# Layer 1's queries, keys and weighed probabilities are turned by VectorE in squares of 32 that change places through memory

## The chip, the cores and the metric

The kernel runs on one core of a Trainium2 chip. The metric is the device time in microseconds (us), as a median over runs: 1236.18 us for the kernel before, over three runs from 1235.33 to 1237.88. Beside it stands one profiled execution, which has a time of its own; all durations below are read from that one.

## The reference, cut to what matters

A two-layer decoder trunk over 512 tokens of 1024 numbers, in float32. Layer 1, where the change is made, has three groups of dilated causal attention with four heads of 128 each, whose outputs are summed per head with weights that come from the softmax denominators:

```python
DIL_PATTERNS = ((128, 1), (512, 4), (2048, 16))
...
    s = jnp.einsum('brhnqd,brhnkd->brhnqk', qc, kb).astype(jnp.float32) * (dh ** -0.5)
...
    s = jnp.where(valid, s, -jnp.inf)
    lse = jax.nn.logsumexp(s, axis=-1)
    p = jnp.exp(s - lse[..., None])
    o = jnp.einsum('brhnqk,brhnkd->brhnqd', p.astype(vb.dtype), vb)
...
    q = rmsnorm(z[:, :, :, 0], q_gain)
    k = rmsnorm(z[:, :, :, 1], k_gain)
    v = z[:, :, :, 2]
...
    wts = jax.nn.softmax(jnp.stack(lses, axis=0), axis=0)
    o = jnp.sum(wts[..., None].astype(v.dtype) * jnp.stack(outs, axis=0), axis=0)
    return o.reshape(B, S, ODD_MIX) @ w_out
```

A gated MLP with a short convolution follows.

## The kernel before, in words

A product on TensorE (PE) takes its contracted index on the partitions. Queries and keys leave their projection with tokens on the partitions and must be turned so that the head's 128 numbers stand there; probabilities leave the softmax with queries on the partitions and must be turned so that keys stand there. The kernel before turns both on PE, 128x128 at a time, against an identity (`cst`), into a PSUM bank, and ScalarE (ACT) copies the bank to SBUF.

All weight products are made of three PE passes (`hi*hi`, `hi*lo`, `lo*hi`). Weights come from memory in slabs: a DMA from SyncE (SP) fills `raw`, ACT makes `hi` (L179), VectorE (DVE) makes `lo` (L182); each has three buffers. A projection of 512 columns is 96 matmuls of 128x512, four slabs of 24; its four tiles of 128 tokens end at six matmuls from each other in the last slab. Layer 1 runs nine such projections one after the other: q and k of group 0, of group 1, of group 2, then the values v0, v1, v2.

The order of PE's instructions is fixed by hand: `at(delay, fn, tag)` puts a piece of work in a heap that comes due after so many us of estimated PE work, and it is placed between the matmuls of the running projection; `drain(tag)` places all that is left. The other engines' instructions are ordered by a scheduler when the program is built; ACT, DVE, GpSimd (POOL) and SP then each go through their own list strictly in order, waits included.

Names and lines that the steps touch:

- `qk_evict` (L383): for each tile, `norm_scale` (square on ACT L367, sum on DVE L369, the root of it by `rsqrt` with two ACT instructions L214 and L215 and small DVE ones), `qn` on DVE (L388), then `tr` 6.5 us and more later: four transposes on PE (L379) and the ACT copy to `q` or `k` (L397, L399). For layer 1 this is 24 tiles.
- `scores` (L876): PE products of `q` and `k`, masks on DVE (L282), exponentials on ACT (L874) into `PR[g]`.
- `residues` and `factors`: small DMAs by POOL (`d`, `s`, `e`, `f`, L913 to L940) and small DVE instructions that give each group's weight per query and head; when they are issued, `weigh` is put into the heap twelve times.
- `weigh` (L943): DVE multiplies each 128x128 block of `PR` in place (L950), then PE transposes it (L957) and ACT copies it back (L959): 60 blocks in 16 banks.
- `values0` (L985): the values of group 0 change their tokens' order through 16 DMAs by POOL (`vt<-vs`).
- `pv` (L962): per head 15 matmuls of the turned blocks with the values (L972), then `split` to `o1hi` and `o1lo` and the output projection (L350).

The profile writes PR, q, k without their group number.

Of the kernel before, what the change touches and what calls it, by code (L numbers as in the profile page):

```python
# [16 lines left out]
F32 = mybir.dt.float32  # L17
F32R = mybir.dt.float32r
I32 = mybir.dt.int32
AF = mybir.ActivationFunctionType  # L20
# [4 lines left out]
P = 128  # L25
# [3 lines left out]
NT = S // P  # L29
# [100 lines left out]
def trunk_kernel(ctx: ExitStack, tc: tile.TileContext, x, weights, params, lqks, w_a2, consts, out):  # L130
    nc = tc.nc
    V, A, G, T = nc.vector, nc.scalar, nc.gpsimd, nc.tensor
# [6 lines left out]
    dr = ctx.enter_context(tc.tile_pool(name="dr", bufs=1, space=bass.MemoryType.DRAM))  # L139
# [3 lines left out]
    def bank():  # L143
        return ps.tile([P, 512], F32, name="bank")
# [7 lines left out]
    ident = cst[:, C_ID:C_ID + P]  # L152
# [122 lines left out]
    g_odd = prm[:, 34:35]  # L275
# [16 lines left out]
    def at(delay, fn, tag):  # L292
        count[0] += 1
        heapq.heappush(events, (now[0] + delay, count[0], tag, fn))

    def fire():
        while events and events[0][0] <= now[0]:
            heapq.heappop(events)[3]()

    def pe(us):  # L300
        now[0] += us

    def run(steps):
        for us in steps:
            pe(us)
            fire()
# [54 lines left out]
    def heads(v, n=4):  # L361
        return v.rearrange("p (h d) -> p h d", h=n)
# [13 lines left out]
    def transposes(src):  # L376
        pt = bank()
        for h in range(4):
            T.transpose(pt[:, h * P:(h + 1) * P], src[:, h * P:(h + 1) * P], ident)  # L379
        pe(0.43)  # L380
        return heads(pt)

    def qk_evict(dst, gain, nh, r, tag, then=None, put=None):  # L383

        def f(t, ps):
            rr = norm_scale(ps, nh, r(t))
            qn = tmp.tile([P, S], F32, name="qn", bufs=3)
            V.tensor_tensor(out=heads(qn, nh), in0=heads(ps, nh),  # L388
                            in1=rr.unsqueeze(2).to_broadcast([P, nh, 512 // nh]), op=ALU.mult)

            def tr():
                pt = transposes(qn)
                to = dst[:, :, t * P:(t + 1) * P]
                if put is not None:
                    to, pt = put(dst, t), pt.rearrange("p h (t l) -> p h t l", t=NT)
                if gain is None:
                    A.activation(to, pt, AF.Copy)  # L397
                else:
                    A.activation(to, pt, AF.Copy, scale=gain)  # L399
                if then is not None:  # L400
                    then(t)
            at(6.5 + t, tr, tag)
        return f

    def scaled(dst, r, c0=0, n=512, then=None):
# [11 lines left out]
    with tc.tile_pool(name="m0", bufs=1) as m0, tc.tile_pool(name="t0", bufs=2) as t0:  # L417
# [145 lines left out]
        def after_k(t):  # L563
            if t == NT - 1:
                at(1.0, lambda: diff_scores(0), "diff")
# [288 lines left out]
    with tc.tile_pool(name="m1", bufs=1) as m1:  # L854
# [8 lines left out]

        PR = [m1.tile([P, 4, 7, P], F32, name="PR0")] + [m1.tile([P, 4, NT, P], F32, name=f"PR{g}") for g in (1, 2)]
        vts = [m1.tile([P, NT, 512], F32, name=f"vt{g}") for g in range(3)]
        fac = []

        def probs(dst, sc, g, t, h):

            nk = sc.shape[1]  # L870
            m = masks[:, 3 - nk // P:3].rearrange("p a b -> p (a b)") if g == 0 else masks[:, 3 * (g - 1)]
            nm = st[g][:, t, 0, h:h + 1]
            masked(dst, sc, m, nm)
            A.activation(dst, dst, AF.Exp, bias=nm, scale=-1.0, accum_out=st[g][:, t, 1, h:h + 1])  # L874

        def scores(g, t, q, k):  # L876
            ts = slice(t * P, (t + 1) * P)
            if g == 0:
                nk = P if t == 0 else 2 * P
                for hp in range(2):  # L880
                    sc = bank()
                    for h in range(2):
                        o = h * 256
                        T.matmul(sc[:, o:o + nk], q[:, 2 * hp + h, ts], k[:, 2 * hp + h, (t + 1) * P - nk:(t + 1) * P],  # L884
                                 start=(h == 0), stop=(h == 1))
                    pe(8 * nk * PASS)
                    for h in range(2):
                        b0 = max(0, 2 * t - 1)
                        dst = PR[0][:, 2 * hp + h, b0:b0 + nk // P].rearrange("p b k -> p (b k)")
                        probs(dst, sc[:, h * 256:h * 256 + nk], 0, t, 2 * hp + h)  # L890
            else:
                sc = bank()
                for h in range(4):
                    hs = slice(h * P, (h + 1) * P)
                    T.matmul(sc[:, hs], q[:, h, ts], k[:, h, ts], start=(h == 0), stop=(h == 3))  # L895
                pe(0.87)
                for h in range(4):
                    probs(PR[g][:, h, t], sc[:, h * P:(h + 1) * P], g, t, h)
            if t < NT - 1:
                at(5.0, lambda: scores(g, t + 1, q, k), "scores")  # L900
            elif g == 0:
                residues()
            elif g == 2:
                factors()
# [13 lines left out]
        def factors():  # L918

            sn = [s0, st[1], st[2]]  # L920
            mx = m1.tile([P, NT, 4], F32, name="mx")
            V.tensor_tensor(out=mx, in0=sn[0][:, :, 0], in1=sn[1][:, :, 0], op=ALU.min)
            V.tensor_tensor(out=mx, in0=mx, in1=sn[2][:, :, 0], op=ALU.min)
            eg = m1.tile([P, 3, NT, 4], F32, name="eg")
            for g in range(3):
                V.tensor_tensor(out=eg[:, g], in0=mx, in1=sn[g][:, :, 0], op=ALU.subtract)
            A.activation(eg.rearrange("p g t h -> p (g t h)"), eg.rearrange("p g t h -> p (g t h)"), AF.Exp)
            den = m1.tile([P, NT, 4], F32, name="den")
            dt = m1.tile([P, NT, 4], F32, name="dt")
            V.tensor_tensor(out=den, in0=eg[:, 0], in1=sn[0][:, :, 1], op=ALU.mult)  # L930
            for g in (1, 2):
                V.tensor_tensor(out=dt, in0=eg[:, g], in1=sn[g][:, :, 1], op=ALU.mult)
                V.tensor_tensor(out=den, in0=den, in1=dt, op=ALU.add)
            V.reciprocal(den, den)
            for g in range(3):
                V.tensor_tensor(out=eg[:, g], in0=eg[:, g], in1=den, op=ALU.mult)

            G.dma_start(e0, eg[:, 0])
            for r in range(4):
                G.dma_start(f0[32 * r:32 * r + 32], e0.rearrange("(t l) r h -> r l t h", t=NT)[r])  # L940
            fac.extend((f0, eg[:, 1], eg[:, 2]))
            for i in range(12):
                at(10.0 + 3.5 * i, lambda i=i: weigh(i // 4, i % 4), "weigh")  # L943

        def weigh(g, h):

            nb = 7 if g == 0 else 4
            for b in range(nb):
                t = (b + 1) // 2 if g == 0 else b
                V.tensor_scalar(PR[g][:, h, b], PR[g][:, h, b], fac[g][:, t, h:h + 1], None, ALU.mult)  # L950

            def tr():
                for b0 in range(0, nb, 4):
                    n = min(4, nb - b0)
                    pt = bank()
                    for b in range(n):
                        T.transpose(pt[:, b * P:(b + 1) * P], PR[g][:, h, b0 + b], ident)  # L957
                    pe(0.107 * n)
                    A.activation(PR[g][:, h, b0:b0 + n].rearrange("p b k -> p (b k)"), pt[:, :n * P], AF.Copy)  # L959
            at(1.5, tr, "weigh")  # L960

        def pv(h):  # L962

            po = bank()
            n0 = po.rearrange("p (t l r) -> p t r l", t=NT, r=4)
            n12 = by_res(po)
            blocks = [(g, b) for g in range(3) for b in range(7 if g == 0 else 4)]
            for i, (g, b) in enumerate(blocks):
                t, kb = ((b + 1) // 2, b // 2) if g == 0 else (b, b)
                to, w = (n0[:, t], PR[g][:, h, b].rearrange("p (r l) -> p r l", r=4)) if g == 0 else \  # L970
                    (n12[:, t], PR[g][:, h, b])
                T.matmul(to, vts[g][:, kb, h * P:(h + 1) * P], w, start=(i == 0), stop=(i == len(blocks) - 1))  # L972
            pe(0.218 * len(blocks))
            return po

# [16 lines left out]
        for g in range(3):  # L992
            q, k = t8("q"), t8("k")
            put = by_tile if g == 0 else None
            run(tok_gemm(512, nat, qk_evict(q, g_odd, 4, rs1, "scores", put=put), make_rs if g == 0 else None))
            run(tok_gemm(512, nat, qk_evict(k, None, 4, rs1, "scores", after_k(g, q, k), put)))
        for g in range(3):
            if g == 2:
                drain("scores")
# [35 lines left out]
```

## Time and profile before

| what | value |
|---|---|
| median of the runs | 1236.18 us (1235.33 to 1237.88) |
| the profiled execution | 1235.43 us |
| its span in the trace | 1233.6 us |
| PE, DVE, ACT, POOL busy | 99%, 62%, 44%, 1% |
| PE's granted clock | full in all 40 slices |

The span runs from the first to the last instruction of the trace; 1.8 us of the execution's time lie around it. In layer 1, the projections of queries and keys begin near 605 us, the last scores end near 788 us, the values of head 0 are gathered from 835 us, and the output projection begins at 848.63 us.

### The profile page before, as it was taken

Reading aid. Unit: us, or ns where it says so; the run is one execution under the profiler, and the core shown is the slowest. Engines: PE = TensorE matmul, PEld = TensorE weight load, DVE = VectorE, ACT = ScalarE, POOL = GpSimd, SP = SyncE. Lnnn points to the kernel's source line nnn. Section 1 sums busy time; section 2 is a strip of 40 time slices with the busy share of each in tenths; the row PEclk is TensorE's granted clock in tenths of the full one; section 3 lists DMA queues with packets and bytes.
Section 4 is the critical chain, followed back from the end, with each engine's and each line's share of the span. In section 5 each row is a group of like instructions: output and inputs, shape, how many; then the busy total and the mean of one; then the engine's idle time right before and its main releaser. Section 6 shows DMA issues by size and latency. Waiting matters only on the chain.

```text
span 1233.6 us, 15017 instructions
## 1 busy us (share of the span) xinstructions
PE 1225.8 (99%) x5783; PEld 1014.4 (82%) x5783; DVE 767.2 (62%) x1450; ACT 546.4 (44%) x896; POOL 16.4 (1%) x35
## 2 busy tenths in 40 slices
PE   9999999999999999999999999999999999999998
PEld 7888688788888888888888888889888888888887
DVE  6557868787744775377645654534777537763673
ACT  6446655454422443245545554444544314432441
POOL 0000000000000000000000000300000000000000
PEclk9999999999999999999999999999999999999999
DMA  7222111233333322332422222421232332332322
GB/s 255 87 87 69 52 53 45 92 94 95 103 94 94 103 97 91 103 94 69 138 86 86 73 83 86 121 85 37 101 102 87 102 103 87 101 103 87 102 77 94
DMA packets 34630, 114.54 MB, mean 93 GB/s; under 512 B 4439, under 2 KB 5368, under 8 KB 34560
## 3 DMA queue, kind: packets, MB, share of 16 engines
q1 hardware_dynamic: 32400, 110.38, 28.4%
q10 hardware_dynamic: 1296, 2.10, 0.5%
q0 software_dynamic: 864, 1.12, 0.4%
q8 instruction: 45, 0.74, 0.2%
q14 instruction: 25, 0.20, 0.1%
HBM read 110.41 MB, written 2.12 MB: 91 GB/s over the span
## 4 chain that ended last, share of the span: by engine, by line
PE 97%; DMA 1%; ACT 1%; DVE 1%; SPq 0%; issue 0%; POOL 0%; DVEq 0%; POOLq 0%; ACTq 0%
PE bank L749 39%; PE bank L333 24%; PE bank L791 19%; PE bank L350 7%; PE bank L379 1%; PE bank L972 1%; PE bank L519 1%; PE bank L553 1%; PE bank L957 1%; PE bank L895 1%; PE bank L884 0%; PE bank L541 0%; PE bank L647 0%; PE bank L681 0%; DMA xT<-in_xT_dram 0%; PE bank L612 0%
## 5 line engine op out<-in xcount | busy, mean ns | idle before, releaser
L179 ACT ACTIVATE hi<-raw 128x1024 fp32r<-128x1024 f32 (+2 forms) x209 | 217.1, 1040 | 310.4 <-PE bank L791 143.2
L182 DVE TENSOR_TENSOR lo<-raw,hi 128x1024 fp32r<-128x1024 f32 (+2 forms) x209 | 250.5, 1199 | 141.0 <-ACT hi L179 134.0
L749 PE MATMUL bank<-hhi,hi 128*128 128x512 f32 x704 | 273.9, 389 | 0.0
L749 PE MATMUL bank<-hhi,lo 128*128 128x512 f32 x704 | 273.9, 389 | 0.0
L749 PE MATMUL bank<-hlo,hi 128*128 128x512 f32 x704 | 273.9, 389 | 0.0
L333 PE MATMUL bank<-hi,hhi 128*128 128x512 f32 (+2 forms) x480 | 186.8, 389 | 0.0
L333 PE MATMUL bank<-lo,hhi 128*128 128x512 f32 (+2 forms) x480 | 181.2, 378 | 0.8 <-DVE lo L182 0.8
L333 PE MATMUL bank<-hi,hlo 128*128 128x512 f32 (+2 forms) x480 | 180.5, 376 | 0.0
L749 PEld LDWEIGHTS bank<-hhi,lo 128*128 128x128 f32 x704 | 132.2, 188 | 27.5
L749 PEld LDWEIGHTS bank<-hlo,hi 128*128 128x128 f32 x704 | 132.2, 188 | 27.4
L749 PEld LDWEIGHTS bank<-hhi,hi 128*128 128x128 f32 x704 | 132.2, 188 | 27.4
L791 PE MATMUL bank<-ghi,lo 128*128 128x512 f32 (+1 forms) x358 | 138.0, 385 | 0.0
L791 PE MATMUL bank<-glo,hi 128*128 128x512 f32 (+1 forms) x358 | 138.0, 385 | 0.0
L791 PE MATMUL bank<-ghi,hi 128*128 128x512 f32 (+1 forms) x358 | 138.0, 385 | 0.0
L333 PEld LDWEIGHTS bank<-lo,hhi 128*128 128x128 f32 x480 | 90.2, 188 | 18.4 <-DVE lo L182 1.5
L333 PEld LDWEIGHTS bank<-hi,hhi 128*128 128x128 f32 x480 | 90.5, 188 | 15.9 <-ACT hi L179 0.6
L333 PEld LDWEIGHTS bank<-hi,hlo 128*128 128x128 f32 x480 | 90.5, 189 | 14.9 <-DVE hlo L207 0.3
L796 DVE TENSOR_TENSOR xT<-xT,bank 128x512 f32<-128x512 f32 (+1 forms) x49 | 33.1, 675 | 106.4 <-PE bank L791 106.2
L791 PEld LDWEIGHTS bank<-ghi,lo 128*128 128x128 f32 x358 | 67.3, 188 | 13.6
L791 PEld LDWEIGHTS bank<-ghi,hi 128*128 128x128 f32 x358 | 67.3, 188 | 13.5
L791 PEld LDWEIGHTS bank<-glo,hi 128*128 128x128 f32 x358 | 67.3, 188 | 13.4
L203 ACT ACTIVATE ghi<-cv 128x512 fp32r<-128x512 f32 x44 | 27.7, 631 | 109.4 <-DVE cv L774 109.4
(201 smaller groups left out, 1340.3 us busy)
## 6 DMA issues: line engine op xcount, KB each, us to landing
raw<-in_weights_dram SPq DMA_DIRECT2D x189, 512.0 KB, 3.5
raw<-in_weights_dram SPq DMA_DIRECT2D x16, 384.0 KB, 3.0
xT<-in_xT_dram SPq DMA_DIRECT2D x7, 256.0 KB, 5.9
out_dram<-xT ACTq DMA_DIRECT2D x7, 256.0 KB, 2.0
raw<-in_weights_dram SPq DMA_DIRECT2D x2, 544.0 KB, 3.5
vt<-vs POOLq DMA_DIRECT2D x16, 64.0 KB, 3.9
raw<-in_weights_dram SPq DMA_DIRECT2D x2, 256.0 KB, 3.1
xT<-in_xT_dram SPq DMA_DIRECT2D x2, 128.0 KB, 3.0
```

What stands on the lines that cost most here:

```text
L179: r = A.activation(hi[:, c0:c1], raw[:, c0:c1], AF.Copy)
L182: V.tensor_tensor(out=lo[:, c0:c1], in0=raw[:, c0:c1], in1=hi.bitcast(F32)[:, c0:c1], op=ALU.subtract)
L203: A.activation(hi, src, AF.Copy)
L333: T.matmul(ps[t][:, :n], lhs(a[:, kc], t), b[:, k, :n], start=(kc == 0 and j == 0), stop=(kc == DC - 1 and j == 2))
L350: T.matmul(ps, w[:, k, d * P:(d + 1) * P], r(k), start=(k == 0 and j == 0), stop=(k == nk - 1 and j == 2))
L379: T.transpose(pt[:, h * P:(h + 1) * P], src[:, h * P:(h + 1) * P], ident)
L519: T.matmul(sc[:, :nk], qT[rs, h, n * P:(n + 1) * P], kT[rs, h, :nk], start=True, stop=True)
L553: T.matmul(po[n][:, h * P:(h + 1) * P], wT[:, j * P:(j + 1) * P], bv[:, j, h * P:(h + 1) * P], start=(h == 0 and j == 0), stop=(h == 3 and ...
L749: T.matmul(ps, w[:, kc], r[:, kc], start=(kc == 0 and m == 0), stop=(kc == DC - 1 and m == 2))
L791: T.matmul(ps[:, ts], a[:, k], b[f0 + k][:, ts], start=(k == 0 and m == 0), stop=(k == n - 1 and m == 2))
L796: V.tensor_tensor(out=xT[:, c, ts], in0=xT[:, c, ts], in1=ps[:, ts], op=ALU.add)
L895: T.matmul(sc[:, hs], q[:, h, ts], k[:, h, ts], start=(h == 0), stop=(h == 3))
```

## The change

Queries, keys and weighed probabilities of layer 1 are no longer turned on PE. `turn` has DVE transpose a tile of 128x512 (or 128x384) inside each square of 32x32, and ACT issues one DMA that writes the result to a buffer in memory. `settle` has POOL issue four DMAs, of 32 partitions each, that read the squares back to the places they have in the turned tile: 128 pieces of 512 (or 384) bytes each. Turned queries and keys arrive in a buffer `z` (three of them), from which ACT copies to `q` and `k` as before; turned probabilities arrive in `PR` itself. The buffer that DVE writes (`turn`) exists twice. What comes due changes with it: the copy to `q` and `k` 11.5 us after the tile and not 6.5, the later scores of group 2 after 4.0 us and not 5.0, and `weigh` in steps of 2.6 us from 6.0 on, head by head (group 1, 2, 0 of head 0, then of head 1, and so on), where it went group by group in steps of 3.5 us from 10.0 on.

```diff
+    def turn(pool, src, n):
+        sq = pool.tile([P, 4, 4, 32], F32, name="turn", bufs=2)[:, :, :n]
+        V.transpose(sq.rearrange("p j b r -> p b j r"), src.rearrange("p (b j c) -> p b j c", b=n, j=4))
+        d = dr.tile([P, 4, n * 32], F32, name=f"turned{n}", bufs=3)
+        A.dma_start(d, sq.rearrange("p j b r -> p j (b r)"))
+        return d.rearrange("(i c) j x -> j c i x", i=4)
+
+    def settle(to, d):
+        for j in range(4):
+            G.dma_start(to[32 * j:32 * j + 32].rearrange("c i b r -> c i (b r)"), d[j])
...
+            if turned is not None:
+                z = turned.tile([P, 4, 4, 32], F32, name="z", bufs=3)
+                settle(z, turn(turned, qn, 4))
+
             def tr():
-                pt = transposes(qn)
...
+                pt = z.rearrange("p i h l -> p h i l") if turned is not None else \
+                    transposes(qn).rearrange("p h (i l) -> p h i l", i=4)
...
-            at(6.5 + t, tr, tag)
+            at((11.5 if turned is not None else 6.5) + t, tr, tag)
...
-                at(5.0, lambda: scores(g, t + 1, q, k), "scores")
+                at(5.0 if g < 2 else 4.0, lambda: scores(g, t + 1, q, k), "scores")
...
             for i in range(12):
-                at(10.0 + 3.5 * i, lambda i=i: weigh(i // 4, i % 4), "weigh")
+                at(6.0 + 2.6 * i, lambda i=i: weigh((1, 2, 0)[i % 3], i // 3), "weigh")
...
-            def tr():
-                for b0 in range(0, nb, 4):
-                    n = min(4, nb - b0)
-                    pt = bank()
-                    for b in range(n):
-                        T.transpose(pt[:, b * P:(b + 1) * P], PR[g][:, h, b0 + b], ident)
-                    pe(0.107 * n)
-                    A.activation(PR[g][:, h, b0:b0 + n].rearrange("p b k -> p (b k)"), pt[:, :n * P], AF.Copy)
-            at(1.5, tr, "weigh")
+            for b0 in range(0, nb, 4):
+                w = PR[g][:, h, b0:min(nb, b0 + 4)].rearrange("p b k -> p (b k)")
+                n = w.shape[1] // P
+                to = w.rearrange("p (i b l) -> p i b l", i=4, b=n)
+                settle(to, turn(m1, w, n))
+                for b in range(n):
+                    turned[g, h, b0 + b] = to[:, :, b]
...
-                T.matmul(to, vts[g][:, kb, h * P:(h + 1) * P], w, start=(i == 0), stop=(i == len(blocks) - 1))
+                T.matmul(to, vts[g][:, kb, h * P:(h + 1) * P], turned[g, h, b], start=(i == 0),
+                         stop=(i == len(blocks) - 1))
...
-            run(tok_gemm(512, nat, qk_evict(q, g_odd, 4, rs1, "scores", put=put), make_rs if g == 0 else None))
-            run(tok_gemm(512, nat, qk_evict(k, None, 4, rs1, "scores", after_k(g, q, k), put)))
+            run(tok_gemm(512, nat, qk_evict(q, g_odd, 4, rs1, "scores", put=put, turned=m1), make_rs if g == 0 else None))
+            run(tok_gemm(512, nat, qk_evict(k, None, 4, rs1, "scores", after_k(g, q, k), put, m1)))
```

Place A: ACT's list where the keys of group 0 are copied, just ahead of the exponentials of the first scores. Before, the four copies come from banks and stand one behind the other:

```order
422 L397 ACTIVATE k<-bank 128x16x32
423 L214 ACTIVATE rs_y_5497<-rs_a_5496 128x4
424 L215 ACTIVATE rs_y_5497<-rs_y_5497 128x4
425 L397 ACTIVATE k<-bank 128x16x32
426 L179 ACTIVATE hi<-raw 128x1024
427 L397 ACTIVATE k<-bank 128x16x32 x2
428 L179 ACTIVATE hi<-raw 128x1024
```

Now, where `z` is the buffer that POOL's DMAs fill:

```order
437 L414 ACTIVATE k<-z 128x16x32
438 L179 ACTIVATE hi<-raw 128x1024
439 L414 ACTIVATE k<-z 128x16x32
440 L367 ACTIVATE sq<-bank,rstd_5160 128x512
441 L214 ACTIVATE rs_y_5678<-rs_a_5677 128x4
442 L215 ACTIVATE rs_y_5678<-rs_y_5678 128x4
443 L414 ACTIVATE k<-z 128x16x32
444 L389 DMA turned_5692<-turn 128x512
```

The last copy of a key tile now stands behind the square `sq` and the root of the first tile of the next queries. On PE the same place reads, now:

```order
2835 L333 MATMUL bank<-hi,hhi 128x512
2836 L333 MATMUL bank<-hi,hlo 128x512
2837 L333 MATMUL bank<-lo,hhi 128x512
2838 L901 MATMUL bank<-k,q 128x128 x4
2839 L333 MATMUL bank<-hi,hhi 128x512
```

The three matmuls ahead of the scores (L901) end the first tile whose `sq` stands ahead of the key copy on ACT; the first scores read all four key tiles, since those of group 0 are stored by residue.

Place D: the end of the values' projection on PE, before (L957 are transposes of weighed probabilities, L972 the gathering of values):

```order
3470 L957 MATMUL bank<-cst,PR_5075 128x128 x4
3471 L333 MATMUL bank<-hi,hhi 128x512
3472 L333 MATMUL bank<-hi,hlo 128x512
3473 L333 MATMUL bank<-lo,hhi 128x512
3474 L333 MATMUL bank<-hi,hhi 128x512
3475 L333 MATMUL bank<-hi,hlo 128x512
3476 L333 MATMUL bank<-lo,hhi 128x512
3477 L957 MATMUL bank<-cst,PR_5075 128x128 x12
3478 L972 MATMUL bank<-PR_5073,vt_5076 128x4x32 x7
```

Now no transpose stands there, and the four heads follow the projection's last matmul:

```order
3443 L333 MATMUL bank<-lo,hhi 128x512
3444 L986 MATMUL bank<-PR_5073,vt_5076 128x4x32 x7
3445 L986 MATMUL bank<-PR_5074,vt_5077 128x128 x4
3446 L986 MATMUL bank<-PR_5075,vt_5078 128x128 x4
3447 L986 MATMUL bank<-PR_5073,vt_5076 128x4x32 x7
3448 L986 MATMUL bank<-PR_5074,vt_5077 128x128 x4
```

POOL's list from the values on, now (`PR_5073` is group 0, `PR_5074` group 1, `PR_5075` group 2; each row is one `settle`, and before the list ended with `f`):

```order
34 L1005 DMA vt_5076<-vs 32x512 x16
35 L955 DMA e_5082<-eg 128x16
36 L957 DMA f_5080<-e_5082 32x4x4 x4
37 L394 DMA PR_5074<-turned_6946 32x4x128 x4
38 L394 DMA PR_5075<-turned_6972 32x4x128 x4
39 L394 DMA PR_5073<-turned_7010 32x4x128 x4
40 L394 DMA PR_5073<-turned_7018 32x4x96 x4
41 L394 DMA PR_5074<-turned_7042 32x4x128 x4
42 L394 DMA PR_5075<-turned_7072 32x4x128 x4
43 L394 DMA PR_5073<-turned_7099 32x4x128 x4
44 L394 DMA PR_5073<-turned_7107 32x4x96 x4
```

The pattern of four rows per head goes on to head 3, and the second half of group 0 is the last of each head, though `pv` reads it among its first rows.

## Rows read from the trace of the kernel before

**Rows 1.** The page: busy us by engine, clock by slice, chain by engine.

```profile
PE 1225.8 (99%) x5783; PEld 1014.4 (82%) x5783; DVE 767.2 (62%) x1450; ACT 546.4 (44%) x896; POOL 16.4 (1%) x35
...
PEclk9999999999999999999999999999999999999999
...
PE 97%; DMA 1%; ACT 1%; DVE 1%; SPq 0%; issue 0%; POOL 0%; DVEq 0%; POOLq 0%; ACTq 0%
```

**Rows 2.** PE's waits: waiter, what it waited for, us in total, times, longest.

```profile
PE bank L224 <- DVE hhi L221: 1.5, 1, 1.5
```

**Rows 3.** Chain of waits, 640 to 700 us: start, us, what.

```profile
639.91 14.75 PE bank L333 x65
654.66 0.44 PE bank L379 x4
...
664.69 0.89 PE bank L884 x8
```

**Rows 4.** Chain of waits, 786 to 872 us, its first row by line.

```profile
by line: PE bank L333 31.8%; PE bank L350 25.3%; PE bank L972 15.6%; PE bank L957 8.5%; DMA f<-e 3.8%; DMA e<-eg 3.5%; POOL f L940 1.9%; PE bank L749 1.8%; ACT PR L874 1.7%; issue 1.6%; DVE lo L182 1.4%; PE bank L895 1.1%; DVE den L933 0.4%
...
786.96 0.90 PE bank L895 x8
...
792.94 3.04 DMA e<-eg
...
796.26 1.65 POOL f L940 x3
797.91 3.25 DMA f<-e
...
801.70 1.50 PE bank L957 x7
...
835.23 13.40 PE bank L972 x120
848.63 21.79 PE bank L350 x96
```

**Rows 5.** Timeline of ACT: start, us, what, idle before.

```profile
625.58 0.69 ACT L367 ACTIVATE sq<-bank,rstd 128x512 f32<-128x512 f32 x1 [0.67 <-PE bank L333]
...
627.75 0.21 ACT L215 ACTIVATE rs_y<-rs_y 128x4 f32<-128x4 f32 x1
```

**Rows 6.** ACT by form, 600 to 850 us: busy us and mean ns of one, idle before.

```profile
L397 ACT ACTIVATE k<-bank 128x512 f32<-128x512 f32 x12 | 7.1, 594 | 13.4 <-PE bank L379 13.4
```

**Rows 7.** DVE by form, 600 to 850 us.

```profile
L182 DVE TENSOR_TENSOR lo<-raw,hi 128x1024 fp32r<-128x1024 f32 x38 | 46.5, 1223 | 76.2 <-ACT hi L179 71.0 <-PE bank L957 5.2
L388 DVE TENSOR_TENSOR qn<-bank,rr 128x512 f32<-128x512 f32 x24 | 16.4, 688 | 0.8
```

**Rows 8.** Timeline of DVE, 792 to 802 us.

```profile
792.51 3.42 DVE L950 TENSOR_SCALAR PR<-PR,eg 128x128 f32<-128x128 f32 x17
```

**Rows 9.** Timeline of POOL, 680 to 830 us.

```profile
778.99 3.96 POOL L990 DMA_DIRECT2D vt<-vs  x8 [85.13 <-ACT vs L988]
```

**Rows 10.** Windows: stretch, its us, PE, PEld, DVE, ACT, POOL busy, clock, DMA, GB/s.

```profile
222.00:224.00 2.00, 1.08 (x4) 0.60 (x5) 1.59 (x2) 0.24 (x1) 0.00 (x0) 1.00 0.04 12
...
224.00:228.00 4.00, 4.00 (x19) 3.28 (x18) 0.93 (x2) 1.00 (x2) 0.00 (x0) 1.00 0.39 125
```

**Rows 11.** Windows while POOL issues four DMAs (`s`, then `f`).

```profile
691.67:693.86 2.19, 2.19 (x12) 1.80 (x11) 0.20 (x1) 0.00 (x0) 2.19 (x4) 1.00 0.37 71
796.26:798.46 2.20, 2.20 (x11) 1.81 (x11) 2.20 (x9) 0.00 (x0) 2.20 (x4) 1.00 0.19 17
```

**Rows 12.** DMA issues: queue, times, KB each, median us to landing.

```profile
xT<-in_xT_dram SPq DMA_DIRECT2D x7, 256.0 KB, 5.9
out_dram<-xT ACTq DMA_DIRECT2D x7, 256.0 KB, 2.0
vt<-vs POOLq DMA_DIRECT2D x16, 64.0 KB, 3.9
...
s<-d POOLq DMA_DIRECT2D x4, 4.0 KB, 5.1
```

More of the change, by code (lines that the diff above doesn't have):

```diff
@@ L381, in transposes, with qk_evict @@
         return heads(pt)
-    def qk_evict(dst, gain, nh, r, tag, then=None, put=None):
+    def turn(pool, src, n):
[7 more added lines that the diff above has]
+            G.dma_start(to[32 * j:32 * j + 32].rearrange("c i b r -> c i (b r)"), d[j])
+    def qk_evict(dst, gain, nh, r, tag, then=None, put=None, turned=None):
         def f(t, ps):
@@ L389, in f @@
                             in1=rr.unsqueeze(2).to_broadcast([P, nh, 512 // nh]), op=ALU.mult)
+            if turned is not None:
+                z = turned.tile([P, 4, 4, 32], F32, name="z", bufs=3)
+                settle(z, turn(turned, qn, 4))
             def tr():
-                pt = transposes(qn)
-                to = dst[:, :, t * P:(t + 1) * P]
-                if put is not None:
-                    to, pt = put(dst, t), pt.rearrange("p h (t l) -> p h t l", t=NT)
+                pt = z.rearrange("p i h l -> p h i l") if turned is not None else \
+                    transposes(qn).rearrange("p h (i l) -> p h i l", i=4)
+                to = put(dst, t) if put is not None else \
+                    dst[:, :, t * P:(t + 1) * P].rearrange("p h (i l) -> p h i l", i=4)
                 if gain is None:
@@ L865, in trunk_kernel @@
         vts = [m1.tile([P, NT, 512], F32, name=f"vt{g}") for g in range(3)]
-        fac = []
+        fac, turned = [], {}
         def probs(dst, sc, g, t, h):
@@ L969, in pv @@
                 t, kb = ((b + 1) // 2, b // 2) if g == 0 else (b, b)
-                to, w = (n0[:, t], PR[g][:, h, b].rearrange("p (r l) -> p r l", r=4)) if g == 0 else \
-                    (n12[:, t], PR[g][:, h, b])
-                T.matmul(to, vts[g][:, kb, h * P:(h + 1) * P], w, start=(i == 0), stop=(i == len(blocks) - 1))
+                to = n0[:, t] if g == 0 else n12[:, t].rearrange("p (i l) -> p i l", i=4)
+                T.matmul(to, vts[g][:, kb, h * P:(h + 1) * P], turned[g, h, b], start=(i == 0),
+                         stop=(i == len(blocks) - 1))
             pe(0.218 * len(blocks))
```

## The prediction

> **What bounds the kernel now.** I read the page first. PE is busy 1225.8 of 1233.6 us and makes 97% of the chain of waits, at the full granted clock (2.4 GHz) in every slice [rows 1]. Its longest wait for anything is 1.5 us, at the start of the first output projection of layer 0 [rows 2]. So the time is the sum of PE's instructions, and what leaves PE leaves the time, unless PE then waits for what came instead. Second, the chain in the projections of layer 1: transposes of a query or key tile stand in it as 0.44 us per four [rows 3]. Third, the chain at the end of the attention: PE again, broken only by the two small DMAs `e` and `f`, during which PE worked on at the values; the weighed probabilities' transposes hold 8.5% of 86.0 us [rows 4]. POOL is nearly idle, 16.4 us in all [rows 1]; the change gives it most of its work, so fourth I read POOL's issues and their landings [rows 9, 11, 12].
>
> **What is removed.** 24 tiles of queries and keys at 0.44 [rows 3]: 10.56 us. The 60 transposes of probabilities: 8.5% of 86.0, 7.3 us [rows 4] (60 at 0.11 would be 6.6; the first group waited for DVE, 1.50 for seven). PE saves 17.9 us, all on the path. ACT loses 16 copies from banks, off the path. The profiled execution took 1235.43, 0.75 below the median of the runs: with nothing late it would become 1217.6, a median of 1218.3.
>
> **What is added, off the path.** DVE gets 40 transposes. The trace has none; an instruction of 128x512 takes 0.69, and four of 128x128 at 0.20 each take 0.8 [rows 7, 8]. I take 0.69, the nearest in shape (bounds 0.2, as one small instruction, and 1.2, as `lo`): 28 us, in an engine idle for 466 [rows 1]. ACT gets 40 DMA issues, each landing perhaps 2.0 after, the time of 256 KB written to memory from ACT's queue [rows 12]. POOL gets four issues per tile: 8 of `vt` took 3.96, 0.495 each, four of `s` 2.19 and of `f` 2.20, 0.55 each [rows 9, 11]. I take 0.55, whose pattern in the buffer has several pieces per partition like the new ones: 2.2 us a tile, 53 for queries and keys and 35 for probabilities. For queries and keys that is 8.8 per projection of 96 matmuls at 0.227 (21.8 us [rows 3]), and the copies come due 5 us later. Cover enough, but for one place.
>
> **Place A, the first scores of group 0.** They read all four key tiles. The last copy stands on ACT behind `sq` and the two root instructions of a tile that PE ends with the very matmul ahead of the scores. From the start of such a `sq` to the end of its second root instruction the trace shows 625.58 to 627.96, 2.4 us [rows 5]; the copy adds 0.6 [rows 6]. PE waits 3.0 (bounds 2.4, if the hand-offs shrink, and 4.2, with one `lo` of 1.2 between on DVE [rows 7]). In groups 1 and 2 the first scores need key tile 0 alone: I find no wait.
>
> **Place D, weighing and gathering.** Let s be the end of the last scores on PE (787.86 before [rows 4]). From there PE has 144 matmuls of the values, 32.7 us, then four heads of 3.35 (13.40 for all [rows 4]), 15 matmuls each. It wants the second half of group 0 after 4 of a head's 15: at s+33.6, 37.0, 40.3 and 43.65.
> - `e` is issued at s+5.1, `f` from s+8.4 and landed at s+13.3 [rows 4]. Group 0 of head 0 can only then be weighed: DVE does five blocks (1.0), a `lo` (1.2), two blocks and the transpose (0.4 and 0.7) [rows 7, 8], then ACT issues and the write lands after 2.0. With hand-offs I put that at s+19.2.
> - POOL has settled groups 1 and 2 of head 0 by then and stood idle some 4 us, because its list has group 0 next. From s+19.2 it has 14 settles of 2.2: head 0 is issued by 23.6, head 1 by 32.4, head 2 by 41.2, head 3 by 50.0. The buffers `turn` don't bind: a transpose, an issue and a landing for two of them are below 2 us a tile.
> - A read of 64 KB lands 3.9 after its issue (`vt`, the same size [rows 12]), so 3.35 after the issue's end: the four heads are complete at 27.0, 35.8, 44.6 and 53.4. Heads 0 and 1 are in time. Head 2 makes PE wait 4.3; head 3, then wanted at 47.95, 5.45 more. Sum 9.75.
>
> ACT also holds the last values' copy behind one DMA issue: 0.3 (0 to 1). After the last head nothing new waits: the output projection begins with heads 0 to 2.
>
> **The sum.** -10.56 - 7.3 + 3.0 + 9.75 + 0.3 = -4.8: 1230.6 beside the profiled 1235.43, a median of 1231.4. For an issue interval i and a landing L the wait at D is 19.2 + 55 i + L - 43.65. Between i 0.495 with L 2.0 and i 0.57 with L 4.5 it is 4.8 to 11.4: 1226 to 1233.
>
> While POOL issued `s`, DVE was busy 0.20 of 2.19 us; while it issued `f`, 2.20 of 2.20, with the weighing itself: four issues took 2.19 and 2.20 [rows 11]. The Trainium skill (SBUF — State Buffer, "SBUF: two separate sides") says that a DMA issued by POOL is starved of descriptors while DVE runs certain SBUF-to-SBUF instructions, and gives 620 ns alone against 3100 beside one. By it, 56 issues would need up to 174 us (an estimate from that page) and the change would be a large loss; this pair of rows shows none of it.
>
> **Rivals.**
> 1. *The queue of eight.* POOL's list lets eight DMAs be under way: each waits for the landing of the one eight before. If L grows, i can't be below L/8. For: a settle moves 128 pieces and `s`, with many small pieces, landed after 5.1; `xT` shows 5.9 when the queues are full [rows 12]. Against: `vt` is as large and took 3.9. At 5.1, i is 0.64, the wait at D 15.7 and the median 1237.3; at 5.9, 0.74, 22.0 and 1243.6. It decides from L = 5.3 on: above, the change is slower by over 0.2%. The Trainium skill (VectorE: DVE Perf Modes, "The three transpose paths") warns of plain DMA copies that transpose by access pattern, 19 times slower than the hardware's own; by it L would be far above 5.9. No run here shows such a copy.
> 2. *The clock falls at place D.* PE idles 2 to 5 us at a time there. For: the trace has no idle so long at full clock. Against: 0.92 us of 2 idle, and the clock stayed at 1.00 there and behind [rows 10]. At the lower level (1.2 GHz) the last 11 gathering matmuls take 2.5 more; a slab of 24 behind them would take 5.5 more. 1233.9 to 1239.4.
> 3. *The settles are hidden*, and only place A waits: i of 0.37 or less, or a walk that starts 10 us earlier. For: nothing in the rows. 1219 to 1225.
> 4. *ACT's list jams.* Its DMA issues wait for DVE and for landings, and `hi` stands behind them. For: 40 new waits in a list kept in order. Against: three buffers of `hi` give PE 8 us and more of slack. Each slab that is late by 2 us costs 2; several, some 6 to 10: 1237 to 1242.
> 5. *POOL starved by DVE* (the same rows speak against it): at most DVE's work in that stretch, some 24 us (14 transposes at 0.69, six `lo`, 35 blocks at 0.20): up to 1255.
>
> **How the numbers follow.** My forecast 0.47 (faster 0.44, within 0.2% 0.03); rival 1 0.23 (within 0.09, slower 0.14); rival 2 0.12 (0.09, 0.03); rival 3 0.10, faster; rival 4 0.05 and rival 5 0.03, slower. Faster 0.54, the same 0.21, slower 0.25; 0.2%, 2.5 us, is about what a measurement of this kernel tells from no change. The range reaches from the middle of rival 3 to the upper end of rival 1: 1222 to 1244.
>
> **What would show it.** PE's waits: the scores of group 0 for ACT's `k`, 3 us; the gathering for POOL's DMAs into PR, near 10 us in heads 2 and 3. POOL's timeline: four issues in 2.2 us, without a pause from the first group 0 on. No rows of L379 in layer 1. The granted clock behind the gathering. I am wrong if POOL's issues there stand apart by more than 0.6 us, if PE doesn't wait at the gathering, or if `lo` or `hi` appear among PE's waits with over 1 us.

## The result, and the profile after

The changed kernel takes 1243.65 us (median of 4 runs, 1241.0 to 1246.0) against 1236.01 for the kernel before, now over four runs: a ratio of 1.0058, 95% interval 1.0046 to 1.0071. It is slower, where 1231.4 and faster was forecast; the time lies inside the stated range. The profiled span grew from 1233.6 to 1241.3 us, by 7.7.

The page after, in the columns of [rows 1]:

```profile
PE 1216.0 (98%) x5627; PEld 1005.4 (81%) x5627; DVE 789.0 (64%) x1490; ACT 538.7 (43%) x880; POOL 103.3 (8%) x195
...
PEclk9999999999999999999998999999999999999999
```

PE lost 156 instructions. Its busy time fell by 9.8 us only, because some of what is left ran at the lower clock; in e10 below, at full clock, it fell by 18.4. PE's waits, where [rows 2] had nothing over 1.5:

```profile
PE bank L901 <- ACT k L414: 6.9, 1, 6.9
PE bank L986 <- DMA PR<-turned: 5.9, 4, 3.1
PE bank L986 <- ACT vt L424: 4.9, 2, 4.0
```

**Place A.** The chain of waits at the first scores of group 0 (start, us, what), against [rows 3]:

```profile
656.86 4.08 DMA turned<-turn
...
663.13 5.70 DMA z<-turned
...
670.07 1.62 POOL z L394 x3
671.69 4.17 DMA z<-turned
675.86 0.02 issue
675.88 0.64 ACT k L414
676.52 0.04 issue
676.56 2.08 PE bank L901 x8
678.64 6.95 PE bank L333 x24
...
694.50 5.45 PE bank L333 x24
```

The last key tile lands at 675.86 and ACT's copy starts at once. On the way POOL's list stood still twice, 1.5 us together, with the next read waiting for the landing of the DMA that had been issued eight before:

```profile
667.76 0.55 POOL L394 DMA_DIRECT2D z<-turned  x1 [0.73 <-DMA z<-turned]
669.11 0.55 POOL L394 DMA_DIRECT2D z<-turned  x1 [0.80 <-DMA z<-turned]
```

Behind the wait the scores take 2.08, where they took 0.89 [rows 3], and the slab behind them 6.95, where later ones take 5.45. The windows there say why (columns as in [rows 10]; the clock is the number after POOL's):

```profile
672.00:676.00 4.00, 0.00 (x0) 0.00 (x0) 3.31 (x8) 1.59 (x5) 0.24 (x1) 0.86 0.75 219
676.00:680.00 4.00, 3.44 (x12) 3.15 (x13) 1.82 (x10) 2.25 (x9) 0.22 (x1) 0.50 0.38 150
680.00:684.00 4.00, 4.00 (x15) 3.21 (x15) 1.05 (x2) 1.38 (x2) 1.95 (x4) 0.78 0.29 70
684.00:688.00 4.00, 4.00 (x20) 3.39 (x19) 3.39 (x17) 2.58 (x9) 0.00 (x0) 1.00 0.11 41
```

While PE idled its clock fell to the lower level (0.50, 1.2 GHz), and from 684 on it read full again. Place A costs 6.9 + 1.2 + 1.5 = 9.6 us; 3.0 was forecast.

**Place D.** PE's timeline, the last scores of group 2 and the gathering (L986):

```profile
793.56 1.05 PE L912 MATMUL bank<-k,q 128*128 128x128 f32 x8
...
827.10 2.62 PE L986 MATMUL bank<-PR,vt 128*128 128x128 f32 x22
833.67 0.80 PE L986 MATMUL bank<-PR,vt 128*128 128x128 f32 x2 [3.95 <-ACT vt L424]
835.46 6.00 PE L986 MATMUL bank<-PR,vt 128*128 128x128 f32 x36 [1.00 <-ACT vt L424]
841.89 1.13 PE L986 MATMUL bank<-PR,vt 128*128 128x128 f32 x8 [0.44 <-DMA PR<-turned]
846.11 4.06 PE L986 MATMUL bank<-PR,vt 128*128 128x128 f32 x22 [3.09 <-DMA PR<-turned]
851.49 1.13 PE L986 MATMUL bank<-PR,vt 128*128 128x128 f32 x8 [1.31 <-DMA PR<-turned]
853.64 2.69 PE L986 MATMUL bank<-PR,vt 128*128 128x128 f32 x22 [1.03 <-DMA PR<-turned]
```

With s at 794.6 the values end at s+32.5 (32.7 worked out). The gathering then takes from 827.1 to 856.3, 29.2 us where 13.40 is its work [rows 4]: 15.8 more, against 10.05 forecast. The clock read 0.66 from 830 to 840, where the 16 DMA engines were busy 0.94 of the time (0.36 in the same stretch before):

```profile
830.00:840.00 10.00, 5.33 (x27) 4.88 (x28) 3.73 (x5) 2.78 (x5) 7.79 (x16) 0.66 0.94 288
```

Between 845 and 850 it read 0.66 again. But the last head's second half starts when its read has landed and runs at full clock, so as this trace reads the falls moved the end little. POOL's timeline, against [rows 9]:

```profile
804.01 1.09 POOL L394 DMA_DIRECT2D PR<-turned  x2
807.48 3.39 POOL L394 DMA_DIRECT2D PR<-turned  x6 [2.38 <-issue]
815.79 4.89 POOL L394 DMA_DIRECT2D PR<-turned  x9 [4.92 <-DMA turned<-turn]
822.09 1.09 POOL L394 DMA_DIRECT2D PR<-turned  x2 [1.42 <-DMA PR<-turned]
...
848.20 3.79 POOL L394 DMA_DIRECT2D PR<-turned  x7 [0.51 <-DMA PR<-turned]
```

It stands idle until group 0 of head 0 has been written (815.79), and then needs 36.2 us for 56 issues, 0.65 each. An issue itself is 0.548, as forecast; nearly all the rest is eight waits for an earlier read's landing, 5.1 us together, and each of them ended within 0.6 us of the landing of the DMA issued eight before. The landings (columns of [rows 12]):

```profile
turned<-turn ACTq DMA_DIRECT2D x36, 256.0 KB, 2.9
z<-turned POOLq DMA_DIRECT2D x96, 64.0 KB, 3.9
PR<-turned POOLq DMA_DIRECT2D x48, 64.0 KB, 4.1
```

The sum by the trace: -17.9 + 9.6 + 15.8 = +7.5 beside the measured 7.7. That the two agree to 0.2 is partly luck: with the 19.1 that e10 shows for the first term the sum would be +6.3.

### The profile page after: what moved, and what is told of

It is laid out like the page before. It is cut to its first block, busy times and chain, and to the rows that moved or that the text cites. A ratio compares the mean times of both kernels' runs of the same rounds, so it can differ in the third digit from the quotient of the medians.

```text
span 1241.3 us, 15085 instructions
## 1 busy us (share of the span) xinstructions
PE 1216.0 (98%) x5627; PEld 1005.4 (81%) x5627; DVE 789.0 (64%) x1490; ACT 538.7 (43%) x880; POOL 103.3 (8%) x195
## 4 chain that ended last, share of the span: by engine, by line
PE 90%; DMA 5%; DVE 2%; POOL 1%; issue 1%; ACT 1%; SPq 0%; DVEq 0%; POOLq 0%; ACTq 0%
PE bank L766 39%; PE bank L808 19%; PE bank L333 18%; PE bank L350 7%; DMA turned<-turn 1%; DMA PR<-turned 1%; DMA z<-turned 1%; PE bank L536 1%; PE bank L570 1%; POOL PR L394 1%; DVE lo L182 1%; PE bank L901 1%; POOL z L394 1%; PE bank L379 1%; PE bank L912 1%
## 5 line engine op out<-in xcount | busy, mean ns | idle before, releaser
L333 PEld LDWEIGHTS bank<-lo,hhi 128*128 128x128 f32 x480 | 90.6, 189 | 17.9 <-DVE lo L182 1.4
L394 POOL DMA_DIRECT2D z<-turned x96 | 52.0, 549 | 516.7 <-DVE rs_a L213 437.5
```

Source lines behind the costliest of these rows:

```text
L333: T.matmul(ps[t][:, :n], lhs(a[:, kc], t), b[:, k, :n], start=(kc == 0 and j == 0), stop=(kc == DC - 1 and j == 2))
L394: G.dma_start(to[32 * j:32 * j + 32].rearrange("c i b r -> c i (b r)"), d[j])
```

## The experiments

Ratios go by the kernel before on the same chip, with the 95% interval in brackets. That kernel took 1236.0 to 1237.4 us in the median on the chips used, so a difference in us between two experiments is good to some 1.5 us. Waits are those of one profiled execution each.

**The parts alone.** e1 takes `weigh` and `pv` from the kernel before, e2 passes no `turned` to `qk_evict`.

```diff
-            run(tok_gemm(512, nat, qk_evict(q, g_odd, 4, rs1, "scores", put=put, turned=m1), ...))   # e2
+            run(tok_gemm(512, nat, qk_evict(q, g_odd, 4, rs1, "scores", put=put), ...))
```

> Only queries and keys go through DVE and memory; the probabilities are weighed and turned as before. Theory (the two places add up: -10.6 of transposes against 9.6 at the first scores, a wait of 6.9 and 2.7 at the lower clock): about -1, 1235, with the same wait of 7 at the first scores of group 0. Rival (the loss at the end of the attention is partly made by the queries' and keys' traffic, or the first scores' wait hides something): under 1232 or over 1239.

> Only the weighed probabilities go through DVE and memory. Theory: -7.3 of transposes against 16 at the gathering: +9, about 1245, with POOL's 56 issues behind the first of group 0 spread over some 36 us. Rival (the first scores' delay is what makes the end late): near 1236.

e1: 1231.16, ratio 0.9957 (0.9943 to 0.9972), with a wait of 6.0 at the first scores. e2: 1239.25, 1.0026 (1.0016 to 1.0036). Queries and keys alone gain 4.9, the probabilities alone lose 3.2, together they lose 7.6: the parts don't add up, and 9 us come from their meeting. The trace of e2 shows the larger part of it. There the last scores end where they did before (787.7), 39.3 us of the values follow them, and the gathering ends at 850.7, 23.8 us after its start:

```profile
786.61 1.05 PE L912 MATMUL bank<-k,q 128*128 128x128 f32 x8
826.95 2.62 PE L986 MATMUL bank<-PR,vt 128*128 128x128 f32 x22
...
837.94 12.78 PE L986 MATMUL bank<-PR,vt 128*128 128x128 f32 x92 [0.73 <-DMA PR<-turned]
```

In the whole change the keys' copies are due 5 us later, 30 matmuls of the values come ahead of the last scores, and the cover for POOL's list (the work on PE between the last scores and the gathering) is 32.5, 6.8 less; the gathering takes 29.2, 5.5 more than in e2. No run changes that cover alone. The expectations for e1 and e2 had taken the places one by one.

**The first scores later.**

```diff
-                    at(2.5 if g == 0 else 1.0, lambda: scores(g, 0, q, k), "scores")
+                    at(8.5 if g == 0 else 1.0, lambda: scores(g, 0, q, k), "scores")
```

> Changed kernel, the first scores of group 0 due 6 us later (one slab of 24 matmuls, 5.46 us, goes ahead of them). Theory T (the last key tile lands late, whatever stands ahead of it): the wait falls from 6.9 to about 1.4, the clock stays at its upper level, 8 us gained: 1235 to 1236. Theory O of the prediction (the copy waits for the square of the tile that PE has just ended): the order moves with it and the wait at the scores stays near 3 or more, or vanishes if ACT's list moves the copy ahead.

> Only queries and keys go through DVE and memory (1231.2 as measured), with the first scores of group 0 due 6 us later. If the 6.0 us wait and the low clock behind it (2 us) are all that place costs, and 1.4 of a new wait comes as in the changed kernel with later scores: 1224 to 1225. If the wait only moves: 1229 or more.

e3: 1236.95, ratio 1.0008 (0.9998 to 1.0018), 6.7 below the changed kernel. The wait for `k` is gone and the clock stays at 1.00; a new one stands among PE's waits:

```profile
PE bank L333 <- DVE qn L401: 1.4, 1, 1.4
```

The clock in the 4 us that hold it:

```profile
676.00:680.00 4.00, 2.56 (x16) 1.97 (x15) 4.00 (x15) 1.79 (x6) 0.53 (x1) 1.00 0.38 98
```

Theory T holds: ACT's copy still starts with the read's landing, 1.3 us after ACT had come free, so the square ahead of it never bound. e8, the same in e1: 1227.36, 0.9923 (0.9908 to 0.9938). That is 9.9 below the kernel before on its chip, where e1 was 4.9 below: 5 more, and not the 6 to 7 expected. The profiled execution (1225.60, a span of 1223.8) comes near the forecast, the median of the runs doesn't, and no trace shows why.

**Whole rows.**

```diff
-        return d.rearrange("(i c) j x -> j c i x", i=4)
+        return d.rearrange("(j c) i x -> j c i x", j=4)
```

> Changed kernel, POOL's reads take whole rows of the buffer in memory, 2 KB a partition in one piece, with the same bytes and the same waits; the squares do not change places, so the output is another. Theory P (the pieces of 512 bytes make the landings long and fill the DMA engines): reads land in 2 to 3 us and not 4, POOL's waits for landings (5.1 us at the end) vanish, the first scores wait 3 to 4 less: 1236 or below. Rival B (bytes and the writes' landings make it): within 2 us of 1243.6.

1242.9, 1.0052 (1.0037 to 1.0067): no change. The reads landed in 3.6 (`z`) and 4.4 (`PR`), against 3.9 and 4.1; POOL still waited 4.0 for landings at the end, in seven waits, and the first scores waited 4.8. Theory P falls: the 512-byte pieces don't make the landings long. The Trainium skill (VectorE: DVE Perf Modes, "The three transpose paths") calls a plain DMA copy that transposes by access pattern 19 times slower than the DMA's own transpose when the innermost stride at its destination is large. Here the innermost run is 512 bytes in one piece, so the warning doesn't reach these reads; the prediction had left out that condition, and no run here shows such a copy.

**Four buffers z.**

```diff
-                z = turned.tile([P, 4, 4, 32], F32, name="z", bufs=3)
+                z = turned.tile([P, 4, 4, 32], F32, name="z", tag="z", bufs=4)
```

> Changed kernel with four buffers z and not three (shared with vs). In the changed kernel POOL's reads of the fourth key tile began 0.5 us after ACT's copy of the first key tile had ended. Theory Z (they wait for that copy, since z has three buffers): they begin when the fourth write has landed, about 1.7 us earlier, the wait at the first scores falls from 6.9 to 5, and the time by 2 to 1241.5. Rival (the landings alone set it): no change.

1243.1, 1.0049 (1.0034 to 1.0064): no change in time. The wait fell to 5.7, but e1 and e6 show 6.0 and 5.9 with three buffers. POOL's last reads of keys now wait for the fourth write:

```profile
668.23 2.17 POOL L394 DMA_DIRECT2D z<-turned  x4 [0.72 <-DMA turned<-turn]
```

Theory Z falls: buffer and write came free within a moment of each other.

**Group 0 last.**

```diff
-                at(6.0 + 2.6 * i, lambda i=i: weigh((1, 2, 0)[i % 3], i // 3), "weigh")
+                at(6.0 + 2.6 * i, lambda i=i: weigh(*((1 + i % 2, i // 2) if i < 8 else (0, i - 8))), "weigh")
```

> Changed kernel, groups 1 and 2 of all heads are weighed before group 0 of any, so that POOL need not wait for the first block of group 0 with nothing to issue. Theory P (POOL's list of 64 issues at about 0.65 us sets the end of the gathering): the last read is issued some 6 us earlier, 1237 to 1238. Rival W (the writes and the two buffers of turn set it, or the waits for the values' copies on ACT): under 2 us gained, or slower.

> The whole change with the first scores of group 0 due 6 us later and group 0 weighed last: the gains of the two alone were 6.7 and 3.8 us. If they add up: 1233. If the earlier last scores only lengthen the wait at the gathering: 1237 or more.

e6: 1239.87, 1.0019 (1.0010 to 1.0029), 3.8 gained, between the two expectations. The waits for `vt` vanish, POOL's last issue is at 846.44 and not 851.4 (1.5 of this because the last scores ended earlier in this execution), and PE waits 9.9 for the reads. e12, with the later first scores as well: 1234.53, 0.9977 (0.9968 to 0.9986): 9.1 of the 10.5 that the two gained alone. The whole change is then a small gain of 0.2%, with 9.5 of waits for reads left.

**Half of the reads from SP.**

```diff
-            G.dma_start(to[32 * j:32 * j + 32].rearrange("c i b r -> c i (b r)"), d[j])
+            (G if j < 2 else nc.sync).dma_start(to[32 * j:32 * j + 32].rearrange("c i b r -> c i (b r)"), d[j])
```

> Changed kernel, two of the four reads of each tile are issued by SP and not by POOL. Theory P (POOL's issues and its limit of eight set the end): the reads of the last head land 10 us earlier, the first scores wait less, 1230 to 1234. Rival D (the DMA engines are full or the landings grow, whoever issues): within 2 us of 1243.6. Rival S (SP's list jams: weight loads stand behind reads that wait for writes): PE waits for lo or hi, slower than 1245.

1241.62, 1.0041 (1.0025 to 1.0056): 2 lower, not 10, and the interval overlaps that of the changed kernel, so no gain is shown. The wait at the first scores did fall, to 3.5, and the last scores ended 2.8 us earlier. But from there to the end of the gathering it took 63.6 us, where the changed kernel took 61.7:

```profile
790.75 1.05 PE L912 MATMUL bank<-k,q 128*128 128x128 f32 x8
...
851.13 4.26 PE L986 MATMUL bank<-PR,vt 128*128 128x128 f32 x22 [3.00 <-issue]
```

POOL issues half as much and now waits for the writes, here in the row of the tile `turned` (who waited, us, times):

```profile
  POOL PR L394: 21.3, 9
```

So a second limit lies right behind POOL's: 16 writes from 802.1 to 841.6, one in 2.6 us, with two buffers `turn` and landings of 2.0 to 6.0, 3.5 in the median. Theory P falls, and rival D had the time, at its edge: its longer landings are in the trace, but the DMA engines were busy 0.68 of 830 to 840 and so not full there.

**Without the trip, and with the writes alone.** e10 leaves out the writes and the reads, e13 the reads; in both the squares do not change places.

```diff
-                settle(z, turn(turned, qn, 4))
+                turn(z, qn, 4)                 # DVE writes z itself
...
+        A.dma_start(d, to.rearrange("p j b r -> p j (b r)"))   # e13 only
```

> Changed kernel without the trip through memory: DVE turns inside the squares of 32 straight into z, and for the probabilities into a buffer that ACT copies back; no write, no read, the squares do not change places. Theory (the saving of 17.9 on PE is whole, and all of the loss comes from the trip): 1218 to 1220, with no wait of PE over 1.5 us. Rival (DVE's 40 transposes cost, or the saving was overcounted): 1224 or more, with PE waiting for lo or for qn.

> The kernel without the trip through memory, plus ACT's 40 writes to memory, which nothing reads; POOL reads nothing back. Theory R (POOL's reads fill the DMA engines and make the writes land late): writes land in 2.0 to 2.2 us, as 256 KB did at the end of the kernel before. Rival W (weight loads and memory make it): 2.8 or more, as in the changed kernel. The time stays within 2 us of 1216 if no read means no wait.

e10: 1216.29, 0.9831 (0.9817 to 0.9846). The saving is whole, 19.1 us in the span, and the time 1.7 below the range expected. PE's longest wait is the old one of 1.5, and a transpose on DVE takes

```profile
L384 DVE STREAM_TRANSPOSE z<-qn 128x512 f32<-128x512 f32 x24 | 16.8, 705 | 0.1
```

0.705 us, where I took 0.69. e13: 1224.11, 0.9903 (0.9887 to 0.9920): 8 us worse than e10 by writes that nobody reads, where I had expected at most 2. Its landings and PE's new wait:

```profile
turned<-z ACTq DMA_DIRECT2D x24, 256.0 KB, 2.2
turned<-turn ACTq DMA_DIRECT2D x12, 256.0 KB, 3.3
```

```profile
PE bank L980 <- ACT vt L416: 4.4, 2, 4.1
```

Spread out, a write lands in 2.2, as forecast; one behind the other at the end, in 3.3 even without a read. There DVE waits 9.6 for `turn` to come free, ACT's next write and its copy back wait for DVE, and the values' copies stand behind those in ACT's list.

**Groups 1 and 2 alone.** e8, with only these two groups' probabilities by DVE and weighed first; group 0 stays on PE.

```diff
+            if g > 0:
+                w = PR[g][:, h].rearrange("p b k -> p (b k)")
+                to = w.rearrange("p (i b l) -> p i b l", i=4, b=4)
+                settle(to, turn(m1, w, 4))
...
+                return
```

> Queries and keys by DVE and memory with the later first scores (1227.4 as measured), and of the probabilities groups 1 and 2 alone, weighed first; group 0, which waits for f, stays on PE. 32 of 60 transposes leave PE, 3.5 to 3.9 us. Theory (what makes the gathering late is that POOL's list is longer than the 33 us that the values give it): 32 issues end some 12 us before PE wants them, 1223.5 to 1224. Rival (any traffic there jams ACT's list and makes PE wait for the values' copies): 1227 or more.

1221.34, 0.9871 (0.9855 to 0.9888): the fastest complete version, 16 us below the kernel before and 2 below what was expected. POOL's last reads, those of head 3, are issued by 819.8, the gathering begins near 822 and takes them last, and PE waits for none:

```profile
817.62 2.17 POOL L394 DMA_DIRECT2D PR<-turned  x4 [0.50 <-DVE lo L182]
```

## Why the prediction was wrong, point by point

The sum came out 12.3 us too low: 6.6 at place A (9.6 and not 3.0) and 5.75 at place D (15.8 and not 10.05). The step that failed is the chain through memory, priced with the landings of lone transfers, a write of 2.0 and a read of 3.9. From it came place A's term, in which the last key tile is in `z` before ACT comes to its copy, and "The buffers `turn` don't bind". Under the change's own traffic a write or a read took up to 6.2 us to land; the last key tile landed some 6 us after PE had begun to wait, and at D the first block of group 0 came later and POOL's list stretched. e10, without the trip, has neither loss.

That the time lies inside the stated range, almost on the 1243.6 of rival 1's upper point, is chance: that point stood for a landing of 5.9 and 22.0 at D.

- **What is removed** was right to 1.2: 17.9 worked out, 19.1 in e10.
- **DVE's part** was right: 0.70 a transpose, hidden.
- **Place A** was named rightly and mis-sized threefold: "PE waits 3.0" measured 6.9, and 2.7 more at the lower clock. The place came out right for another reason. I took the copy to be held by the square and roots ahead of it in ACT's list; it was held by the tile's landing (675.86). I had used the write's landing of 2.0 and the read's of 3.9; on the chain they are 4.1, then 5.7 and 4.2. ACT's list delayed the start as well: `hi` and the first square of the keys stood behind a copy of queries that waited for its read (ACT's timeline below, with the idle time before in brackets). And POOL's list had its part: with half of the reads issued by SP (e7) the wait was 3.5. e3 and e8 show the wait go when the scores come later.

```profile
647.80 0.72 ACT L416 ACTIVATE q<-z,prm 128x512 f32<-128x512 f32 x1 [1.96 <-DMA z<-turned]
648.42 1.04 ACT L179 ACTIVATE hi<-raw 128x1024 fp32r<-128x1024 f32 x1
649.37 0.67 ACT L367 ACTIVATE sq<-bank,rstd 128x512 f32<-128x512 f32 x1
```

- **The clock** was a rival at place D alone. It cost its 2.7 at place A, where the prediction gave it no price; at D it fell too, behind waits that set the end anyway.
- **Place D** was the right mechanism with the size off: 15.8 against 10.05. Group 0 of head 0 could be read at s+21.2 and not s+19.2, since its write landed after 4.2 and not 2.0 us; 56 issues took 36.2 and not 30.8; the last landing, 2.0, gave 1.9 back.
- **Rival 1, the queue of eight**, had its place and sign right: 0.65 us an issue, between its two priced points (and over the 0.6 that I had named as a sign of being wrong), and in the trace its 5.1 us of waits are the largest part of what I missed at D. That it alone made D late is not shown: e7 halves POOL's list and gains nothing there. Its 15.7 at D for a landing of 5.1 is met by chance, since the reads landed in 4.1 in the median and the last in 2.0. The small pieces were not the cause (e4).
- **"The buffers `turn` don't bind"** failed: below 2 us a tile was worked out with a landing of 2.0. In the changed kernel DVE waited 13.1 us for them behind the last scores, e7 shows 2.6 a tile, and e13 the loss that writes and buffers make without a read.
- **Rival 4, ACT's list**, was put down to `hi`. It was `vt`: 4.9 us of waits here, 4.4 in e13.
- **The sum** had the short cover of 32.7 us right, but not as a price of the queries' and keys' part: their later copies take 6.8 us of it, and the gathering is 5.5 longer than in e2, the larger part of the 9 by which e1 and e2 don't add up.
- **Rival 5** is refuted: 64 issues at 0.548 in the median beside a DVE that worked. The rule of the Trainium skill (SBUF — State Buffer, "SBUF: two separate sides"), 620 ns alone and 3100 beside certain DVE instructions, is not seen beside the weighing, the `lo` and the transposes that DVE ran here:

```profile
L394 POOL DMA_DIRECT2D PR<-turned x64: 548/548/656, 804.0 to 851.4; - x64
```

What stays open: why writes one behind the other land in 3.3 and more with no read beside them (weight loads go on there, and were not taken away); how much of D is POOL's queue, how much the writes, and how much DMA engines that are nearly full (0.94 busy from 830 to 840; but in e7 0.68 there, without a gain, and in e11 0.96 from 805 to 815, without a wait of PE for a read); and why e8's median lies 1.8 above its profiled execution.

## What to carry to other kernels

A trip through memory that replaces work on the bounding engine must be priced as a chain: buffers, issue and landings under the load that the change itself makes, not the landing of a lone transfer. Divide that chain by the buffers and compare it with the cover behind the last input. Move the part whose cover is long (here queries, keys, and the two groups that need no late factor) and leave the rest where it was: e11 keeps 16 of the 21 us that e10 shows to be there. And a wait of some us on PE is to be priced with the lower clock behind it.

## What the runs showed of the hardware

- Over the 6.9 us without work before 676.56 PE's clock began to fall (0.86 from 672 to 676); it read 0.50 in the next 4 us and 1.00 from 684 on; the price was 2.7 us. In e3, with a wait of 1.4, it stayed at 1.00.
- Pieces of 512 bytes or rows of 2 KB: the same landing for 64 KB, 3.9 and 4.1 against 3.6 and 4.4.
- Four reads of 64 KB in pieces of 512 bytes cost POOL 2.17 or 2.18 us to issue where nothing held them, with DVE at work beside them; an issue took 0.548 in the median, and 0.498 with rows of 2 KB (e4).
- A write of 256 KB landed in 2.2 when writes came one by one, and in 3.3 one behind the other, both without reads (e13).
